# Two attention mixers re-ordered: pool products, window sums, scores, values and the first output products

## The chip, the cores and the metric

The kernel runs on one core of a Trainium2 chip. It is one launch, and the metric is its time on the device in microseconds (us). A core has engines that work side by side, each through its own queue in program order: TensorE (PE) for matrix products, VectorE (DVE), ScalarE (ACT) and GpSimd (POOL) for work on tiles, and SyncE (SP), whose queue issues the transfers of weights from memory. An instruction that needs the result of another engine waits on a semaphore, and everything behind it on its own engine waits with it. PE writes into PSUM, of which the kernel uses 8 banks of 128 x 512 numbers; all other tiles lie in SBUF.

## The reference

Two networks run one after the other on 512 tokens of width 1024. The change touches the mixers of the first network alone. It has two layers (DEPTH 2); each begins with a mixer block and ends with a gated feed-forward block:

```python
for l in range(DEPTH):
    h = rms_norm(x, g_mix_norm[l])
    z = h @ w_in[l]
    q_lat, kv_lat, k_rope, uv, pin = parts of z (256, 128, 32, 512, 256 wide)
    a  = mla_mixer(q_lat, kv_lat, k_rope, ...)     # 4 heads, causal softmax, values of 128 per head
    gm = sgu_mixer(uv, ...)                        # u * (causal 128x128 product over time of rms_norm(v) + b)
    po = pool_mixer(pin, w_pool[l], pool_scale[l])
    mix = concatenate([rms_norm(a, g), rms_norm(gm, g), rms_norm(po, g)])
    x = x + mix @ w_out[l]
    h = rms_norm(x, g_ffn_norm[l])
    x = x + (silu(h @ w_gate[l]) * (h @ w_up[l])) @ w_down[l]
```

`pool_mixer` takes four groups of 64 channels. Group g has a window of 2, 4, 8 or 16 tokens: the mean over the window (over fewer tokens at the start) minus the input, times a 64 x 64 matrix of the group, times a scale.

## The kernel before

All activations are kept turned: a tile holds 128 channels on its partitions and the 512 tokens along its free side. A weight product is made of three matmuls of 512 columns (lines 195 to 197): the weight and the activation are each split into a high and a low part, and high-high, low-high and high-low are added up in PSUM. Such a triple is called a product here. A weight arrives as a raw tile by a transfer of SP (three raw tiles at most), ACT makes its high part (L157) and DVE its low part (L158); the two together are a unit, of which five are alive at most. `plan_all` lists the units in the order in which they are wanted, and `get` and `done` split a few units ahead of the one in use. So a unit's place in the list also sets where its two splits stand in the queues of ACT and DVE.

`mixer(l)` writes out the order of everything else by hand, and each engine's queue is the order in which the code runs. It goes in stages:

1. The loop over four blocks of 128 tokens, `for b in range(4)`, makes q, k and v (lines 928 to 937, 18 matmuls of 384 columns for each b). ACT scales q and v out of PSUM (L940, L944), DVE scales k (L943), and ACT and POOL square them for their norms.
2. `pool_in(0)` scales the first pool tile (L959), and POOL forms its window sums by doubling shifts (L964, L965): a shifted addition and a short copy for each doubling. DVE then runs a reciprocal square root as a chain of ten small instructions (L978, then lines 247 to 256) for q, scales q, turns it by the rotary angles (lines 986 to 991) and splits three units.
3. PE meanwhile makes the 288 wide products (v of the gate and the rotary part of k, lines 1001 to 1003), then steps of the two gate tiles by `filler`, each step two products. `heads(0)` turns q and k of head 0 (L1055). ACT scales them out of PSUM (L1059).
4. The score loop: 16 items (h, b), head by block of queries, and 20 steps. Step i makes the score of item i (L1155) with its softmax (DVE maximum with mask L1158, ACT exponential L1162), scales the probabilities of item i-1 (L1170), turns those of item i-3 (L1178, evacuated by ACT at L1181) and multiplies item i-4 by v (L1194, a matmul of 128 columns for each pair of blocks). `side` hangs other work on steps: the eight steps of `second` (the product for the second pool tile, lines 195 to 197) in steps 0 to 3, the gate's spatial products, heads 1 to 3, `pool_mean` and `pool_out` (L1115) for the two pool tiles, and the norms of the gate tiles gm and the pool tiles po.
5. The output: six PSUM banks, first the products of gm and po (`mix[4:8]`) into the first two pairs, then those of the attention.

## Time and profile before

| what | value |
| --- | --- |
| median of 3 runs | 2565.69 us (2565.5 to 2567.38) |
| the profiled execution | 2565.37 us |
| its span in the trace | 2563.6 us |
| PE busy | 2538.0 us, 99% |
| DVE, ACT, POOL busy | 50%, 34%, 20% |
| mean granted clock of PE | 0.997 |
| mixer of layer 0 in the trace | about 20 to 145 us |
| mixer of layer 1 in the trace | about 541 to 650 us |

The span is from the first to the last instruction of the profiled execution; 1.8 us of its time lie outside. The timeline gives the start and length of an instruction or a group of like ones, and in brackets how long its engine sat idle before it and whose instruction ended that. A matmul's length overlaps the next one's, so the pace of PE is read from the distance of starts. In the windows view a clock of 1.00 means that the full 2.4 GHz was granted all the time; the lower level is 1.2 GHz.

### The profile page before, as it was taken

Reading aid. Unit: us, or ns where it says so; the run is one execution under the profiler, and the core shown is the slowest. Engines: PE = TensorE matmul, PEld = TensorE weight load, DVE = VectorE, ACT = ScalarE, POOL = GpSimd, SP = SyncE. Lnnn points to the kernel's source line nnn. Section 1 sums busy time; section 2 is a strip of 40 time slices with the busy share of each in tenths; the row PEclk is TensorE's granted clock in tenths of the full one; section 3 lists DMA queues with packets and bytes.
Section 4 is the critical chain, followed back from the end, with each engine's and each line's share of the span. In section 5 each row is a group of like instructions: output and inputs, shape, how many; then the busy total and the mean of one; then the engine's idle time right before and its main releaser. Section 6 shows DMA issues by size and latency. Waiting matters only on the chain.

```text
span 2563.6 us, 30126 instructions
## 1 busy us (share of the span) xinstructions
PE 2538.0 (99%) x12237; PEld 2106.6 (82%) x12237; DVE 1275.3 (50%) x1937; ACT 870.9 (34%) x1285; POOL 506.4 (20%) x409
## 2 busy tenths in 40 slices
PE   9999999999999999999999999999999999999998
PEld 7788888887888888888888888888888888888887
DVE  6855343468553434545433435653544445344345
ACT  5543232245432323323322334422222234233243
POOL 5412010124120101211330001252423331000011
PEclk9999999999999999999999999999999999999999
DMA  5032333220333232323333222423222213323321
GB/s 152 26 124 99 99 102 102 78 81 26 124 99 99 99 99 83 99 99 107 100 102 108 90 96 78 120 83 83 83 82 83 83 50 108 102 94 99 99 74 58
DMA packets 265219, 235.03 MB, mean 92 GB/s; under 512 B 9022, under 2 KB 262744, under 8 KB 265080
## 3 DMA queue, kind: packets, MB, share of 16 engines
q1 hardware_dynamic: 264264, 231.97, 28.9%
q8 instruction: 96, 1.57, 0.3%
q10 hardware_dynamic: 752, 1.12, 0.1%
q14 instruction: 43, 0.35, 0.0%
q0 software_dynamic: 64, 0.01, 0.0%
HBM read 230.98 MB, written 2.10 MB: 91 GB/s over the span
## 4 chain that ended last, share of the span: by engine, by line
PE 95%; DVE 1%; ACT 1%; issue 0%; DVEq 0%; ACTq 0%
PE ps L195 28%; PE ps L197 28%; PE ps L196 28%; PE v L1335 1%; PE v L1337 1%; PE v L1336 1%; PE ps L1361 1%; PE o L1394 1%; PE rows L287 1%; PE ps L1383 1%; PE o L1404 0%; PE ps L1357 0%; PE ps L1194 0%; PE ps L1155 0%; PE st L280 0%; PE ps L280 0%
## 5 line engine op out<-in xcount | busy, mean ns | idle before, releaser
L195 PE MATMUL ps<-h,wh 128*128 128x512 f32 x3248 | 1271.2, 391 | 0.7 <-ACT wh L157 0.7
L197 PE MATMUL ps<-h,wl 128*128 128x512 f32 x3248 | 1264.8, 389 | 1.4 <-DVE wl L158 1.4
L196 PE MATMUL ps<-l,wh 128*128 128x512 f32 x3248 | 1264.0, 389 | 0.1
L158 DVE TENSOR_TENSOR wl<-raw,wh 128x1024 fp32r<-128x1024 f32 (+4 forms) x466 | 579.6, 1253 | 837.0 <-ACT wh L157 835.2
L157 ACT ACTIVATE wh<-raw 128x1024 fp32r<-128x1024 f32 (+4 forms) x466 | 449.9, 986 | 1027.0 <-PE ps L196 984.4
L197 PEld LDWEIGHTS ps<-h,wl 128*128 128x128 f32 x3248 | 609.7, 188 | 130.5 <-DVE wl L158 2.7
L195 PEld LDWEIGHTS ps<-h,wh 128*128 128x128 f32 x3248 | 609.8, 188 | 127.5 <-issue 1.8
L196 PEld LDWEIGHTS ps<-l,wh 128*128 128x128 f32 x3248 | 610.0, 188 | 125.7 <-DVE l L234 0.5
L320 POOL TENSOR_TENSOR sq<-sq,sq 128x512 f32<-128x512 f32 x68 | 92.3, 1357 | 748.7 <-ACT sq L271 748.4
L679 POOL TENSOR_TENSOR th<-th,half 128x512 f32<-128x512 f32 x44 | 83.0, 1906 | 554.8 <-DVE th L678 554.8
L1307 POOL TENSOR_TENSOR sw<-sw,trig 32x512 f32<-32x512 f32 x48 | 74.8, 1559 | 286.9 <-DVE sw L1306 268.3
L647 DVE TENSOR_TENSOR x<-x,ps 128x512 f32<-128x512 f32 x144 | 97.9, 702 | 9.4 <-PE ps L197 9.4
L236 ACT ACTIVATE h<-x,vec 128x512 fp32r<-128x512 f32 x72 | 56.0, 778 | 102.4 <-DVE x L647 96.3
L234 DVE TENSOR_TENSOR l<-r,h 128x512 fp32r<-128x512 f32 x64 | 44.3, 693 | 88.0 <-ACT h L233 86.5
L237 DVE SCALAR_TENSOR_TENSOR l<-x,vec,h 128x512 fp32r<-128x512 f32 x72 | 58.0, 805 | 55.2 <-ACT h L236 55.1
L709 ACT ACTIVATE r<-r 128x512 f32<-128x512 f32 x64 | 40.5, 632 | 101.5 <-DVE r L708 101.5
L1314 POOL TENSOR_TENSOR qk<-qk,sw 32x512 f32<-32x512 f32 x32 | 59.5, 1860 | 2.5
L1370 ACT ACTIVATE P<-P,s 128x512 f32<-128x512 f32 (+1 forms) x32 | 22.1, 693 | 88.7 <-DVE s L1368 88.7
L1335 PE MATMUL v<-wh,h 128*128 128x512 f32 x128 | 51.0, 399 | 0.0
L271 ACT ACTIVATE sq<-x 128x512 f32<-128x512 f32 x79 | 48.8, 618 | 6.3 <-DVE x L728 6.3
L1337 PE MATMUL v<-wh,l 128*128 128x512 f32 x128 | 50.0, 390 | 0.0
L1336 PE MATMUL v<-wl,h 128*128 128x512 f32 x128 | 49.9, 389 | 0.0
(268 smaller groups left out, 1661.7 us busy)
## 6 DMA issues: line engine op xcount, KB each, us to landing
raw<-in_attn_w_qkv SPq DMA_DIRECT2D x72, 512.0 KB
raw<-in_mlp_w_up SPq DMA_DIRECT2D x32, 1024.0 KB
raw<-in_mlp_w_down SPq DMA_DIRECT2D x32, 1024.0 KB
raw<-in_w_gate SPq DMA_DIRECT2D x22, 1024.0 KB
raw<-in_w_up SPq DMA_DIRECT2D x22, 1024.0 KB
raw<-in_w_down SPq DMA_DIRECT2D x16, 1024.0 KB
raw<-in_sc_w_in SPq DMA_DIRECT2D x12, 1024.0 KB
raw<-in_w_out SPq DMA_DIRECT2D x16, 512.0 KB
```

The costliest lines, as they stand in the source:

```text
L157: nc.scalar.activation(out=hi, in_=raw, func=AF.Copy)
L158: nc.vector.tensor_tensor(out=lo, in0=raw, in1=hi.bitcast(F32), op=ALU.subtract)
L195: mm(out=ps, lhsT=wh, rhs=xh, start=start, stop=False)
L196: mm(out=ps, lhsT=wh, rhs=xl, start=False, stop=False)
L197: mm(out=ps, lhsT=wl, rhs=xh, start=False, stop=stop)
L320: nc.gpsimd.tensor_tensor(out=self.acc, in0=self.acc, in1=sq, op=ALU.add)
L647: self.nc.vector.tensor_tensor(out=x, in0=x, in1=ps, op=ALU.add)
L679: nc.gpsimd.tensor_tensor(out=t[i], in0=t[i], in1=half, op=ALU.mult)
L1307: pool.tensor_tensor(out=sw[0:32], in0=sw[0:32], in1=sinr, op=ALU.mult)
L1335: pe.matmul(out=pss[r], lhsT=xh, rhs=hi[:, k, :], start=first, stop=False)
L1336: pe.matmul(out=pss[r], lhsT=xh, rhs=lo[:, k, :], start=False, stop=False)
L1337: pe.matmul(out=pss[r], lhsT=xl, rhs=hi[:, k, :], start=False, stop=last)
```

## The change

In each of the two mixers:

- The unit of the second pool tile is planned ahead of the 288 wide units, and its eight products run in the q/k/v loop, two behind each b. The 24 matmuls leave the score loop.
- `pool_in(0)`, `pool_in(1)` and all window sums stand right behind the loop. POOL now has 14 instructions there instead of 4: in the last doubling of a tile the two halves of the partitions go apart, one as a copy of 64 x 512 (L974 of the new file), the other as an addition.
- `pool_mean` works on whole tiles (one DVE instruction of 128 x 512 and two short ones of POOL for each pool tile, instead of twice that on halves) and stands on DVE between the splits and the norm of k. `pool_out(0)` stands on PE ahead of the last three gate steps before `heads(0)`, `pool_out(1)` right ahead of `heads(0)`.
- The score's maximum becomes a minimum of the scaled and negated scores, so that the small DVE instruction between it and the exponential goes. The probabilities of the last block of queries are scaled by ACT instead of DVE.
- Probabilities are turned six steps behind their score instead of three, by block of keys: `turn(h, c)` takes block c of all later query blocks, and `values(h, c)` is one matmul of (4-c) x 128 columns. That makes 16 instead of 40 matmuls for a layer, with as many columns. The loop has 23 steps.
- The square of the attention output goes from POOL to ACT. The norms of gm and po share one chain on DVE (step 8), with the scaling and splitting of gm and po in steps 11 to 14 (before: 15 to 19).
- The first pair's products of gm and po (four steps of two products) stand in steps 16, 18, 20 and 22; the second pair's stand half ahead of and half behind the column sums of the attention's norm.

The diff, cut:

```diff
                 self.mm(ps, (hi[:, k, :], lo[:, k, :]), xs[k], start and k == 0, stop and k == n - 1)
         self.done(*[u for u, _, _ in us])
 
-    def pair_steps(self, pss, xs):
+    def pair_steps(self, pss, xs, stop=True):
 
         us = [self.get() for _ in pss]
         n = len(xs)
         for k in range(n):
             for ps, (u, hi, lo) in zip(pss, us):
...
             self.plan([(a["w_kv_up"][l], 0, 768)], 0, 1, [(0, 768)])
+            self.plan([(w, 1056, 128)], 0, 8, [(0, 128)])
             for k0, nk in ((0, 3), (3, 3), (6, 2)):
                 self.plan([(w, 672, 256), (w, 384, 32)], k0, nk, [(0, 288)])
             self.plan_cols(w, 8, 416, 256)
-            self.plan([(w, 1056, 128)], 0, 8, [(0, 128)])
...
+        pps.append(self.bank())
+        pool_steps = self.pair_steps(pps[1:], xs)
         for b in range(4):
...
             v.tensor_reduce(out=ssk[:, b * 4:b * 4 + 4], in_=t4, op=ALU.add, axis=mybir.AxisListType.X)
+            next(pool_steps)
+            next(pool_steps)
         self.done(uq, uk)
...
-            ss_ = [t]
-            for sh in ((1, 2), (1, 2, 4, 8))[i]:
-                s, o = self.T(name="sum"), ss_[-1]
-                pool.tensor_tensor(out=s[:, sh:], in0=o[:, sh:], in1=o[:, :512 - sh], op=ALU.add)
-                pool.tensor_copy(out=s[:, 0:sh], in_=o[:, 0:sh])
-                ss_.append(s)
-            sums.append(ss_[-2:])
...
+        def pool_sums(i):
+
+            o = pin[i]
+            win = ((1, 2), (1, 2, 4, 8))[i]
+            for sh in win:
+                s = self.T(name="sum")
+                last = sh == win[-1]
+                if last:
+                    pool.tensor_copy(out=s[0:64], in_=o[0:64])
+                p = slice(64, 128) if last else slice(0, 128)
+                pool.tensor_tensor(out=s[p, sh:], in0=o[p, sh:], in1=o[p, :512 - sh], op=ALU.add)
+                pool.tensor_copy(out=s[p, 0:sh], in_=o[p, 0:sh])
+                o = s
+            sums.append(o)
 
         pool_in(0)
+        pool_in(1)
+        pool_sums(0)
+        pool_sums(1)
...
-        gate_steps = self.pair_steps(ups, xs)
-
-        def second():
-            pps.append(self.bank())
-            yield from self.pair_steps(pps[1:], xs)
-
-        fill = [gate_steps] * 8 + [second()] * 8
+        fill = [self.pair_steps(ups, xs)] * 8
...
+        mm_ = []
+
+        def pool_mean(i):
+            m, s, c = self.T(name="m"), sums[i], i * 17
+            v.scalar_tensor_tensor(out=m, in0=s, scalar=self.counts[:, c + 16:c + 17], in1=pin[i], op0=ALU.mult, op1=ALU.subtract)
+            pool.tensor_tensor(out=m[:, 0:16], in0=s[:, 0:16], in1=self.counts[:, c:c + 16], op=ALU.mult)
+            pool.tensor_tensor(out=m[:, 0:16], in0=m[:, 0:16], in1=pin[i][:, 0:16], op=ALU.subtract)
+            mm_.append(m)
...
+        def pool_out(i):
+            ps = self.bank()
+            pe.matmul(out=ps, lhsT=pb[:, i * 128:(i + 1) * 128], rhs=mm_[i], start=True, stop=True)
+            t = self.T(name="po")
...
+        pool_mean(0)
+        pool_mean(1)
...
+        pool_out(0)
         filler(3)
+        pool_out(1)
         heads(0)
         filler(1)
...
+        def stats():
             ps = self.bank()
...
+            for c, j in ((0, "g"), (4, "p")):
+                self.columns(sgp[j], ps, c)
+            var = self.small(8)
+            v.tensor_scalar(out=var, in0=ps[:, 0:8], scalar1=1.0 / 256, scalar2=EPS, op0=ALU.mult, op1=ALU.add)
+            both = self.rsqrt(var)
+            fac["g"], fac["p"] = both[:, 0:4], both[:, 4:8]
...
-            mx, sm = self.small(1), self.small(1)
-            v.tensor_tensor_reduce(out=t[:, 0:n], in0=ps[:, 0:n], in1=self.causal[:, 512 - n:512], scale=1.0, scalar=-3e38,
-                                   op0=ALU.add, op1=ALU.max, accum_out=mx)
-            self.tick()
-            v.tensor_scalar(out=mx, in0=mx, scalar1=-scale, scalar2=None, op0=ALU.mult)
-            act.activation(out=t[:, 0:n], in_=t[:, 0:n], func=AF.Exp, scale=scale, bias=mx, accum_out=sm)
+            mn, sm = self.small(1), self.small(1)
+            v.tensor_tensor_reduce(out=t[:, 0:n], in0=ps[:, 0:n], in1=self.causal[:, 512 - n:512], scale=-scale, scalar=3e38,
+                                   op0=ALU.add, op1=ALU.min, accum_out=mn)
+            act.activation(out=t[:, 0:n], in_=t[:, 0:n], func=AF.Exp, scale=-1.0, bias=mn, accum_out=sm)
...
             v.reciprocal(out=sm, in_=sm)
-            self.tick()
-            v.tensor_scalar(out=t[:, 0:n], in0=t[:, 0:n], scalar1=sm, scalar2=None, op0=ALU.mult)
-            self.tick()
-
...
+            if b < 3:
+                v.tensor_scalar(out=t[:, 0:n], in0=t[:, 0:n], scalar1=sm, scalar2=None, op0=ALU.mult)
+            else:
+                act.activation(out=t[:, 0:n], in_=t[:, 0:n], func=AF.Copy, scale=sm)
...
-            for c in range(b + 1):
-                pe.transpose(blk(ps, c), blk(t, c), self.ident)
+            for b in range(c, 4):
+                pe.transpose(blk(ps, b), blk(prob[h, b][0], c), self.ident)
+            prob.pop((h, c))
...
-        def values(h, b):
-            if b == 0:
+        def values(h, c):
+            if c == 0:
...
-            t = ptt.pop((h, b))
-            for c in range(b + 1):
-                pe.matmul(out=blk(outs[h], b), lhsT=v4[:, c, h, :], rhs=blk(t, c), start=c == 0, stop=c == b)
-            if b == 3:
+            t = ptt.pop((h, c))
+            pe.matmul(out=outs[h][:, c * 128:], lhsT=v4[:, c, h, :], rhs=t[:, c * 128:], start=c == 0, stop=c == 3)
+            if c == 3:
...
-                s = self.T(name="sq")
-                pool.tensor_tensor(out=s, in0=o, in1=o, op=ALU.mult)
+                s = self.square(outs[h])
...
-                    pool.tensor_tensor(out=sa[0], in0=sa[0], in1=s, op=ALU.add)
+                    (v if h == 3 else pool).tensor_tensor(out=sa[0], in0=sa[0], in1=s, op=ALU.add)
...
-        side = {0: lambda: filler(3), 1: lambda: (filler(1), pool_mean(0)), 2: lambda: (filler(1), heads(1)),
-                3: lambda: (filler(3), pool_out(0)), 4: lambda: (filler(1), spatial(0), gate(0)),
-                5: lambda: (pool_in(1), spatial(1)), 6: lambda: gate(1),
-                7: lambda: (heads(2), pool_mean(1), squares(gm)), 8: lambda: heads(3), 10: lambda: pool_out(1),
-                11: lambda: stats("g"), 14: lambda: (stats("p"), rowsof("g")),
-                15: lambda: (scaled(gm, "g", v), rowsof("p")), 17: lambda: parts(gm, 4, "g_out_sgu"),
-                18: lambda: scaled(po, "p", v), 19: lambda: parts(po, 6, "g_out_pool")}
-        for i in range(len(items) + 4):
+        pss = []
+
+        def output(n):
+
+            if not pss:
+                pss.extend([self.bank(), self.bank()])
+                fill.extend([self.pair_steps(pss[0:2], mix[4:8], stop=False)] * 4)
+            filler(n)
+
+        side = {0: lambda: spatial(0), 1: lambda: (spatial(1), gate(0)), 2: lambda: (heads(1), gate(1)),
+                3: lambda: squares(gm), 6: lambda: heads(2), 8: stats, 9: lambda: heads(3),
+                10: lambda: (rowsof("g"), rowsof("p")), 11: lambda: scaled(gm, "g", v), 12: lambda: parts(gm, 4, "g_out_sgu"),
+                13: lambda: scaled(po, "p", v), 14: lambda: parts(po, 6, "g_out_pool")}
+        for i in range(len(items) + 7):
+            if 0 <= i - 6 < len(items):
+                turn(*items[i - 6])
             if i < len(items):
                 score(*items[i])
             if 0 <= i - 1 < len(items):
                 scale_p(*items[i - 1])
-            if 0 <= i - 3 < len(items):
-                turn(*items[i - 3])
-            if 0 <= i - 4 < len(items):
-                values(*items[i - 4])
+            if i in (16, 18, 20, 22):
```

On PE, layer 0, around the turning of head 0 (`ps`: PSUM tiles, `h` and `l`: parts of an activation, `wh` and `wl`: parts of a unit, `m`: the pool mean, `pb`: the pool matrix). Before:

```order
L197 MATMUL ps_831<-h_275,wl_678 128x512
L1055 MATMUL ps_918<-ident,q_562 96x128 x4
L1055 MATMUL ps_925<-ident,k_563 96x128 x4
L195 MATMUL ps_830<-h_285,wh_673 128x512
L196 MATMUL ps_830<-l_286,wh_673 128x512
L197 MATMUL ps_830<-h_285,wl_674 128x512
L195 MATMUL ps_831<-h_285,wh_677 128x512
L196 MATMUL ps_831<-l_286,wh_677 128x512
L197 MATMUL ps_831<-h_285,wl_678 128x512
L1155 MATMUL ps_951<-kT_930,qT_923 128x128
L195 MATMUL ps_959<-h_158,wh_796 128x512
```

The change:

```order
L197 MATMUL ps_876<-h_275,wl_709 128x512
L1043 MATMUL ps_979<-m_927,pb_360 128x512
L1089 MATMUL ps_986<-ident,q_562 96x128 x4
L1089 MATMUL ps_993<-ident,k_563 96x128 x4
L195 MATMUL ps_875<-h_285,wh_704 128x512
L196 MATMUL ps_875<-l_286,wh_704 128x512
L197 MATMUL ps_875<-h_285,wl_705 128x512
L195 MATMUL ps_876<-h_285,wh_708 128x512
L196 MATMUL ps_876<-l_286,wh_708 128x512
L197 MATMUL ps_876<-h_285,wl_709 128x512
L1168 MATMUL ps_1017<-kT_998,qT_991 128x128
L1117 MATMUL ps_1024<-wT_741,vn_1011 64x128 x4
```

`pool_out(1)` now stands ahead of the turning (and `pool_out(0)` 18 rows above it), and behind the first score come the spatial products instead of the second pool tile's.

On POOL behind the q/k/v loop (`pin`: pool tile, `sum`: window sums, `kr`, `kp`: rotary part of k). Before:

```order
L964 TENSOR_TENSOR sum_683<-pin_681 128x511
L965 COPY sum_683<-pin_681 128x1
L964 TENSOR_TENSOR sum_686<-sum_683 128x510
L965 COPY sum_686<-sum_683 128x2
L1035 TENSOR_TENSOR kr_860<-kr_860,s_551 128x64 x4
L1036 TENSOR_TENSOR kp_861<-kr_860 128x4x16
L1037 TENSOR_TENSOR kp_861<-kr_860 128x4x16
L1109 TENSOR_TENSOR m_982<-sum_683,counts 64x16
L1110 TENSOR_TENSOR m_982<-m_982,pin_681 64x16
```

The change, from the fourth of its instructions there:

```order
L976 TENSOR_TENSOR sum_719<-sum_716 64x510
L977 COPY sum_719<-sum_716 64x2
L976 TENSOR_TENSOR sum_723<-pin_714 128x511
L977 COPY sum_723<-pin_714 128x1
L976 TENSOR_TENSOR sum_726<-sum_723 128x510
L977 COPY sum_726<-sum_723 128x2
L976 TENSOR_TENSOR sum_729<-sum_726 128x508
L977 COPY sum_729<-sum_726 128x4
L974 COPY sum_732<-sum_729 64x512
L976 TENSOR_TENSOR sum_732<-sum_729 64x504
L977 COPY sum_732<-sum_729 64x8
L1035 TENSOR_TENSOR m_923<-sum_719,counts 128x16
```

All sums of both tiles, ten instructions more, and the first tile's short means now stand ahead of the work on k.

On DVE in the last steps with a score, 12 to 14 (`P`: probabilities, L1171: the minimum, L1154: scaling of gm and po, L237: low part of an activation). Before, at the end of the scores:

```order
L1168 RECIPROCAL s_1348<-s_1348 128x1
L1170 TENSOR_SCALAR P_1346<-P_1346,s_1348 128x384
L1141 TENSOR_TENSOR gm_1075<-gm_1075,rows_1391 128x512
L1141 TENSOR_TENSOR gm_1121<-gm_1121,rows_1391 128x512
L1168 RECIPROCAL s_1397<-s_1397 128x1
L1170 TENSOR_SCALAR P_1395<-P_1395,s_1397 128x512
L237 SCALAR_TENSOR_TENSOR l_1443<-gm_1075,vec,h_1442 128x512
L237 SCALAR_TENSOR_TENSOR l_1447<-gm_1121,vec,h_1446 128x512
L1141 TENSOR_TENSOR po_1045<-po_1045,rows_1423 128x512
L1141 TENSOR_TENSOR po_1265<-po_1265,rows_1423 128x512
L237 SCALAR_TENSOR_TENSOR l_1472<-po_1045,vec,h_1471 128x512
L237 SCALAR_TENSOR_TENSOR l_1476<-po_1265,vec,h_1475 128x512
```

The change:

```order
L1171 ISA P_1290,s_1291<-ps_1288,causal 128x128
L1171 ISA s_1291 128x1
L1179 RECIPROCAL s_1274<-s_1274 128x1
L237 SCALAR_TENSOR_TENSOR l_1299<-gm_1033,vec,h_1298 128x512
L237 SCALAR_TENSOR_TENSOR l_1303<-gm_1053,vec,h_1302 128x512
L1171 ISA P_1312,s_1313<-ps_1310,causal 128x256
L1171 ISA s_1313 128x1
L1179 RECIPROCAL s_1292<-s_1292 128x1
L1181 TENSOR_SCALAR P_1290<-P_1290,s_1292 128x128
L1154 TENSOR_TENSOR po_957<-po_957,rows_1262 128x512
L1154 TENSOR_TENSOR po_981<-po_981,rows_1262 128x512
L1171 ISA P_1331,s_1332<-ps_1329,causal 128x384
```

The scaling and splitting of gm and po stood behind the last maximum and now stand between the minima of head 3.

## Rows read from the trace of the kernel before

**Rows 1.** Page, part 4: shares of the chain that ended last.
```profile
PE 95%; DVE 1%; ACT 1%; issue 0%; DVEq 0%; ACTq 0%
```

**Rows 2.** Windows view, us from:to, length, busy (x instructions), clock, DMA, GB/s.
```profile
100.00:120.00 20.00, 18.02 (x123) 14.69 (x124) 15.84 (x63) 11.81 (x33) 10.27 (x12) 1.00 0.00 1
...
600.00:620.00 20.00, 17.35 (x119) 13.74 (x116) 16.28 (x43) 11.23 (x30) 14.64 (x19) 0.91 0.09 27
```

**Rows 3.** Waits of PE in layer 0's mixer: waiter, releaser, total us, times, longest.
```profile
PE ps L1194 <- ACT PT L1181: 2.8, 5, 1.4
PE ps L1155 <- ACT kT L1059: 2.0, 1, 2.0
PE ps L1055 <- DVE k L1047: 0.9, 1, 0.9
PE ps L935 <- ACT q L940: 0.5, 1, 0.5
PE ps L935 <- ACT v L944: 0.4, 1, 0.4
```

**Rows 4.** The same view, layer 1's mixer: its first line.
```profile
PE ps L1194 <- ACT PT L1181: 2.6, 4, 1.4
```

**Rows 5.** Timeline of PE: start us, us, what [idle before]; first products of stages.
```profile
42.08 0.42 PE L928 MATMUL ps<-wh,h 128*128 128x384 f32 x1
...
52.99 0.40 PE L1001 MATMUL ps<-wh,h 128*128 128x288 f32 x1
...
555.66 0.43 PE L928 MATMUL ps<-wh,h 128*128 128x384 f32 x1
...
564.46 0.38 PE L1001 MATMUL ps<-wh,h 128*128 128x288 f32 x1
...
577.29 0.40 PE L195 MATMUL ps<-h,wh 128*128 128x512 f32 x1
...
586.86 0.38 PE L1055 MATMUL ps<-ident,q 128*96 128x128 f32 x2
```

**Rows 6.** Timeline of DVE behind the q/k/v products, layer 0, last row layer 1.
```profile
61.84 0.69 DVE L978 TENSOR_SCALAR s<-s 128x16 f32<-128x16 f32 x1
...
62.77 1.01 DVE L249 TENSOR_TENSOR s<-s 128x16 f32<-128x16 f32 x1
...
63.81 0.18 DVE L250 TENSOR_TENSOR s<-s,s 128x16 f32<-128x16 f32 x1
...
65.28 1.76 DVE L981 TENSOR_TENSOR q<-q,s 128x1536 f32<-128x1536 f32 x1
...
69.51 2.80 DVE L158 TENSOR_TENSOR wl<-raw,wh 128x1024 fp32r<-128x1024 f32 x3
...
572.42 0.70 DVE L978 TENSOR_SCALAR s<-s 128x16 f32<-128x16 f32 x1
```

**Rows 7.** Timeline of POOL in layer 0: its second addition.
```profile
62.71 1.04 POOL L964 TENSOR_TENSOR sum<-sum 128x510 f32<-128x510 f32 x1
```

**Rows 8.** Timeline of ACT in layer 0's score loop.
```profile
107.08 0.68 ACT L271 ACTIVATE sq<-ps,vec 128x512 f32<-128x512 f32 x1
...
108.28 0.72 ACT L1162 ACTIVATE P<-P,s 128x512 f32<-128x512 f32 x1 [0.51 <-DVE s L1161]
```

**Rows 9.** Timeline of DVE in layer 0's score loop.
```profile
79.62 1.66 DVE L1071 SCALAR_TENSOR_TENSOR vn<-ps,s,gb 128x256 f32<-128x256 f32 x4
...
118.97 1.29 DVE L1141 TENSOR_TENSOR gm<-gm,rows 128x512 f32<-128x512 f32 x2
...
121.81 1.97 DVE L237 SCALAR_TENSOR_TENSOR l<-gm,vec,h 128x512 fp32r<-128x512 f32 x2 [0.38 <-ACT h L236]
```

**Rows 10.** Timeline of PE: layer 0's keys turned; its first output product; layer 1's score (1,0).
```profile
76.93 0.61 PE L1055 MATMUL ps<-ident,k 128*96 128x128 f32 x4 [0.91 <-DVE k L1047]
...
123.84 0.47 PE L195 MATMUL ps<-h,wh 128*128 128x512 f32 x1
...
610.55 0.49 PE L1155 MATMUL ps<-kT,qT 96*128 96x128 f32 x2 [2.04 <-ACT kT L1059]
```

More of the change, by code (lines that the diff above doesn't have):

```diff
@@ L220, in pair_steps @@
             for ps, (u, hi, lo) in zip(pss, us):
[L221 removed]
+                self.mm(ps, (hi[:, k, :], lo[:, k, :]), xs[k], k == 0, stop and k == n - 1)
             if k < n - 1:
@@ L1217, in mixer @@
                 scale_p(*items[i - 1])
-            if 0 <= i - 3 < len(items):
-                turn(*items[i - 3])
-            if 0 <= i - 4 < len(items):
-                values(*items[i - 4])
+            if i in (16, 18, 20, 22):
+                output(1)
+            if 0 <= i - 7 < len(items):
+                values(*items[i - 7])
             if i in side:
                 side[i]()
-        pss = [self.bank() for _ in range(6)]
-        self.pair(pss[0:2], mix[4:8], stop=False)
+        pss += [self.bank() for _ in range(4)]
+        steps = self.pair_steps(pss[2:4], mix[4:8], stop=False)
+        next(steps)
+        next(steps)
         sps = self.bank()
@@ L1231, in mixer @@
         ca = self.rsqrt(var)
-        self.pair(pss[2:4], mix[4:8], stop=False)
+        next(steps)
+        next(steps)
         row = self.rows(ca)
```

52 lines of the change are left out of this document (13 added, 39 removed).

## The prediction

> **What bounds the kernel now.** I read the page's chain first: PE holds 95% of it [rows 1], and its clock is nearly full, so the change can save only time in which PE waits or runs slow. The windows show where: in 100 to 120 us PE is busy 18.02 of 20, in 600 to 620 it is busy 17.35 with a granted clock of 0.91, that is partly at 1.2 and mostly at 2.4 GHz [rows 2]. DVE is busy 16 of 20 there, so the loop is short of slack, not of DVE throughput. The waits view then names what PE waits for. Layer 0: turned probabilities 2.8, keys out of ACT 2.0, k out of DVE 0.9, the q/k/v loop 0.5 + 0.4 [rows 3]. Layer 1: 2.6 [rows 4], and 2.0 before the first score of head 1 [rows 10].
>
> **What can be gained.** The q/k/v loop of layer 0 takes 52.99 - 42.08 = 10.91 us, in layer 1 564.46 - 555.66 = 8.80 [rows 5], so its waits with their small gaps are worth 2.1. With the 0.9 before k and 4.8 in the score loop layer 0 holds 7.8. Layer 1 holds 4.6, and the low clock in 600 to 620 costs 20 x 0.09 = 1.8: together 6.4. If all of this went and nothing came, 14.2 us would be saved, 0.55%.
>
> **Work that only moves.** A product takes (586.86 - 577.29) / 14 = 0.68 us, since 14 stand between these two rows [rows 5]. The eight pool products are 5.47 wherever they stand, and so are the eight output products pulled into steps 16 to 22. Value matmuls become fewer but have the same columns, and the rows of the loop go by columns; I take zero. The two pool_out matmuls only leave the loop. POOL's square of the attention and DVE's 512 wide scaling go to ACT, which is busy 11.8 of 20 in 100 to 120 [rows 2] and hides them except in the late steps below. The moved weight unit reorders splits and transfers, with no more of either; layer 0's loop starts some 0.25 us later for the larger split ahead of it, covered by the products inside. Tail and merged norms: the two halves of the second output pair are 2.7 us each and cover a chain of ten small DVE steps (0.21 each, from 63.81 to 65.28 in seven [rows 6]); zero.
>
> **Step 1, the q/k/v loop: -2.1.** ACT and DVE set its pace in layer 0. Two products behind each b put 1.37 us of PE work where it waited. Layer 1 had no wait, so nothing there.
>
> **Step 2, pool_out(0) ahead of heads(0): +4.2 and +2.3.** PE reaches it after 8.80 + 5.47 + 12.83 (the 288 wide products, 564.46 to 577.29 [rows 5]) + 5.47 (four gate steps) = 32.6 us: at 74.6 in layer 0. What it needs is the last of a long DVE queue. That chain began at 61.84 before [rows 6]; a second pool_in (some 0.6), a 576 wide split that now comes behind the loop (some 0.9) and the later start of the loop put it at about 63.8. Without hindrance: chain 2.1, q and rotation 4.2 (65.28 to 69.51), three splits of 512 some 2.1 (2.80 is for four such widths [rows 6]), the mean and its two short POOL steps 1.3, so 73.5, before PE comes. But POOL now has six additions, two half copies and six short copies there, about 9 us, to 71.5. While one runs, DVE's small steps stand still: 0.69 and 1.01 instead of 0.18 [rows 6], each ending with an addition of 1.04 [rows 7]; between two additions about two steps get through. Ten steps then need five additions with their copies at 1.25 each, 6.3 instead of 2.1, and q waits for the last addition, 1.1 more. The mean is there at 73.5 + 4.2 + 1.1 = 78.8, PE waits 4.2. Bounds: 0, if the copies leave DVE free, and 6.0, if DVE's long steps also hold POOL up. In layer 1 the chain began at 572.42, 16.8 us behind the first product against 19.8 in layer 0 [rows 5, 6], but DVE must now follow a loop 5.47 longer, which gives back 1.1 of the 3.0: 2.3, bounds 0 and 4.2. Behind it on PE wait three gate steps and head 0; no other engine is short of them.
>
> The Trainium skill ("SBUF — State Buffer", Who interferes with whom) says that a VectorE instruction with two SBUF inputs and a GpSimd instruction that reads SBUF exclude each other, and that whichever began holds the other up for its whole length. The blocked rows agree; that POOL is held up too no row of this stretch shows, since its additions keep their 1.04. By the full rule step 2 would be at its upper ends, 6.0 + 4.2, and the total 3.7 us more.
>
> **Step 3, k of head 0: +0.9 each, -0.9 in layer 0.** With 4 us more of PE work ahead of it, k is ready when PE comes, so the old 0.9 [rows 3] goes. But its turning takes a PSUM bank that pool_out(1) just filled, and that ACT frees after a scaling and a square of 0.68 each at most [rows 8], less 0.43 of q's turning: 0.8 to 1.1.
>
> **Step 4, the start of the score loop: +4.4 each.** Before, pool products stood between the first scores; now nothing does. The spatial products wait for vn, a split and 1.66 us on DVE [rows 9], against 2.8 us at most since k's turning: 1.5. Score (1,0) waits for k of head 1 behind three exponentials on ACT: 1.8 by the queue order, near the 2.0 that the same wait had [rows 3]. turn(0,0) needs the score (0,3) of three PE entries earlier to pass maximum, exponential (0.72 [rows 8]), reciprocal and ACT's scaling: 1.1. Bounds 3 and 5.
>
> **Step 5, the late steps: +4.8 each.** Before, gm and po were scaled and split behind the last maximum. Now the four scalings (1.29 for two) and four low parts (1.97 for two [rows 9]), 6.5 us of DVE, stand between the minima of head 3, with four high parts and two norm rows on ACT among its exponentials. Minima and scalings of head 3 are some 3.5 us more, so DVE has 10 us in steps 11 to 14, in which PE has some 7 of scores, turns and values. PE waits at values (1,1), (1,3), (2,0), (2,1), (2,2) and at turn(2,0): following the three queues by the rows' lengths I find 0.65 + 0.65 + 0.85 + 2.25 + 1.65 + 0.4 = 6.4. Such a walk misses short gaps on both sides: before's loop, 46.9 us from 76.93 to 123.84 [rows 10], is 3.3 longer than its matmuls and waits added up. I count half of that against the 6.4: 4.8, bounds 2.6 (DVE's excess alone) and 6.4.
>
> **Sum.** Layer 0: -2.1 + 4.2 - 0.9 + 0.9 + 4.4 + 4.8 - 4.8 (the loop's old waits) = +6.5. Layer 1: 2.3 + 0.9 + 4.4 + 4.8 - 4.6 - 1.8 = +6.0. The profiled execution has 2565.4 us, its span 2563.6 and 1.8 outside; 2565.4 + 12.5 = 2577.9, and with the median 0.3 above it, **2578**. All terms at their lower ends give -1.4 and 0: 2564. All at their upper ends, with the clock dip staying: +10.7 and +12.1: 2588.
>
> **Rivals.** *The old waits go and few new ones come (faster).* Turning six steps behind gives the softmax twice the time, the cause of most waits in rows 3 and 4. If the copies leave DVE free (step 2: 0) and the late queues drain inside the six steps (step 5: 0), with step 4 at the spatial wait alone, 1.5: layer 0 +2.4 - 7.8, layer 1 +2.4 - 6.4: 2565.7 - 9.4 = 2556. It decides from new waits under 7.1 us a layer. For it: the lag is generous for heads 0 to 2, and the small step behind the maximum is gone. Against it: DVE's blocked steps are in the trace, and the late work is queued ahead of the exponentials that the last turns need.
>
> *About no change.* Step 2 near zero, the loop's new waits just replacing the old: 2562 to 2570.
>
> *The clock falls behind the new waits.* A wait of 2.04 left the clock at 1.00 in 100 to 120, while in layer 1 the same wait stands in the window with 0.91 [rows 2, 3, 10]. The waits of step 2 and 5 may each cost such a 1.8: two to four of them make 2582 to 2585. The Trainium skill ("TensorE: Matmul & The Clock Gate", HAM oscillation) has waits in a loop throttle PE again and again; these rows show it in one of two cases.
>
> *The change doesn't do what it says:* the pool products might still trail the loop if their unit came late; its transfer starts where that of a 288 wide unit did, so I give that nothing of its own.
>
> **Chances.** Forecast 0.45, low clock 0.22, about no change 0.2, faster rival 0.13. A difference under 0.2%, 5.1 us, is about what a measurement of this kernel can't tell from none, so same is 2560.6 to 2570.8. The forecast's lower tail falls into it: faster 0.13, same 0.22, slower 0.65. The range leaves out the faster rival and the worst: 2561 to 2588.
>
> **What would show it.** Right: PE idle some 4 us before L1043 in layer 0 and 2 in layer 1, released by POOL or DVE; POOL additions back to back with DVE's chain stretched to 6 us beside them; no wait left at L935; waits at the values matmul in the last head's steps. Wrong: a chain of 2 us beside the sums, or the pool mean there before PE; a first score row without waits; values without waits from step 12 on. A q/k/v loop of over 15 us would mean that the moved unit came late.

## The result: 0.7% slower

| | before | the change |
|---|---|---|
| median, us | 2566.53 (2565.5 to 2568.17) | 2585.66 (2580.3 to 2587.12) |
| profiled execution, us | 2565.37 | 2586.89 |
| its span, us | 2563.6 | 2585.1 |
| mean granted clock of TensorE (PE) | 0.997 | 0.993 |

The ratio is 1.0072, with a 95% interval of 1.0059 to 1.0084: slower, and clear of the 0.2% that the prediction took as the least that such a measurement can tell. The forecast was 2578, the range 2561 to 2588.

The chain that ended last, in the page of the changed kernel (part 4), holds what [rows 1] did not: DVE with three per cent and POOL with one.

```profile
PE 94%; DVE 3%; ACT 1%; POOL 1%; issue 1%; DMA 0%; ACTq 0%; DVEq 0%; POOLq 0%
```

The waits view of the changed kernel, for PE, layer 0's mixer (waiter, releaser, total us, times, longest):

```profile
PE ps L1202 <- ACT PT L1192: 4.1, 4, 1.7
PE ps L1043 <- POOL m L1036: 3.6, 1, 3.6
PE ps L1189 <- ACT P L1183: 1.3, 2, 1.1
PE ps L1168 <- ACT kT L1093: 1.2, 1, 1.2
PE ps L1117 <- DVE vn L1107: 1.1, 1, 1.1
PE ps L1089 <- ACT sq L271: 0.9, 1, 0.9
```

Of the five waits of [rows 3] those on k, q and v are gone, those on PT and kT now stand at other products, and four are new: 12.2 us against 6.6. In layer 1 the six are the same, but for 1.7 at L1043: 10.3 against the 4.6 of [rows 4, 10]. Waits thus grew by 11.3. The timeline of PE (start, length, what, idle before) says where they lie:

```profile
42.39 0.42 PE L930 MATMUL ps<-wh,h 128*128 128x384 f32 x1
...
57.04 0.38 PE L1016 MATMUL ps<-wh,h 128*128 128x288 f32 x1
...
79.14 1.13 PE L1043 MATMUL ps<-m,pb 128*128 128x512 f32 x2 [3.63 <-POOL m L1036]
...
88.18 0.64 PE L1089 MATMUL ps<-ident,k 128*96 128x128 f32 x4 [0.92 <-ACT sq L271]
...
120.95 0.33 PE L1189 MATMUL ps<-ident,P 128*128 128x128 f32 x1 [0.26 <-ACT P L1183]
...
122.34 0.49 PE L1202 MATMUL ps<-PT,v 128*128 128x128 f32 x2 [0.41 <-ACT PT L1192]
...
124.47 1.12 PE L1202 MATMUL ps<-PT,v 128*128 128x512 f32 x2 [0.46 <-ACT PT L1192]
...
128.80 0.91 PE L1202 MATMUL ps<-PT,v 128*128 128x384 f32 x2 [1.59 <-ACT PT L1192]
...
131.49 1.22 PE L1202 MATMUL ps<-PT,v 128*128 128x256 f32 x2 [1.66 <-ACT PT L1192]
...
567.45 0.43 PE L930 MATMUL ps<-wh,h 128*128 128x384 f32 x1
...
581.82 0.38 PE L1016 MATMUL ps<-wh,h 128*128 128x288 f32 x1
```

From the first q product of layer 0 to that of layer 1 it is 567.45 - 42.39 = 525.1 us, where [rows 5] have 513.6: layer 0 became 11.5 longer. What follows, 2585.1 - 567.45 = 2017.7 against 2007.9, became 9.7 longer. That is some 10 us more than the growth of the waits, and the windows view (from:to, length, busy by engine, granted clock, DMA share, GB/s) shows it:

```profile
80.00:100.00 20.00, 16.66 (x90) 11.39 (x88) 12.44 (x36) 8.07 (x18) 5.66 (x9) 0.91 0.09 26
100.00:120.00 20.00, 18.82 (x96) 13.87 (x96) 10.05 (x42) 13.27 (x34) 2.85 (x3) 0.83 0.00 1
120.00:140.00 20.00, 15.62 (x62) 10.24 (x61) 8.10 (x20) 11.76 (x28) 2.56 (x2) 0.91 0.00 1
...
620.00:640.00 20.00, 18.71 (x102) 14.16 (x102) 11.33 (x47) 14.11 (x37) 4.11 (x4) 0.91 0.01 1
640.00:660.00 20.00, 15.62 (x57) 10.21 (x55) 8.10 (x20) 11.41 (x27) 2.56 (x2) 0.83 0.00 0
```

Here 100 to 120 has a busier PE than in [rows 2], 18.82 against 18.02, and gets less done: its clock is 0.83 instead of 1.00. At 20 us for each share of clock that is missing, layer 0 loses 20 x (0.09 + 0.17 + 0.09) = 7.0 and layer 1 20 x (0.09 + 0.17) = 5.2, where before lost 1.8 [rows 2]: 10.4 more. Finer windows of the same kernel show stretches near half speed (1.2 GHz), each behind PE's idle time:

```profile
76.00:80.00 4.00, 0.86 (x3) 0.49 (x3) 3.79 (x13) 0.00 (x0) 1.61 (x6) 1.00 0.41 131
80.00:84.00 4.00, 4.00 (x12) 3.03 (x11) 3.22 (x8) 1.27 (x2) 1.31 (x5) 0.57 0.00 0
...
100.00:104.00 4.00, 2.92 (x11) 2.04 (x11) 2.42 (x8) 2.64 (x7) 2.85 (x3) 0.58 0.01 4
```

So the 21.5 us between the two spans are about half waits and half clock. The second half is an estimate from the windows; the first run below tests it. The clock varies from run to run: the changed kernel's run of 2580.3 us had a mean of 0.996, those of 2584.4, 2586.9 and 2587.1 had 0.993.

### The profile page after: what moved, and what is told of

Its sections match the earlier page's. It is cut to its first block, busy times and chain, and to the rows that moved or that the text cites. A ratio compares the mean times of both kernels' runs of the same rounds, so it can differ in the third digit from the quotient of the medians.

```text
span 2585.1 us, 29866 instructions
## 1 busy us (share of the span) xinstructions
PE 2546.5 (99%) x12141; PEld 2103.5 (81%) x12141; DVE 1257.5 (49%) x1875; ACT 881.2 (34%) x1301; POOL 492.4 (19%) x395
## 4 chain that ended last, share of the span: by engine, by line
PE 94%; DVE 3%; ACT 1%; POOL 1%; issue 1%; DMA 0%; ACTq 0%; DVEq 0%; POOLq 0%
PE ps L195 28%; PE ps L197 28%; PE ps L196 28%; PE v L1353 1%; PE v L1355 1%; PE v L1354 1%; PE ps L1379 1%; PE o L1412 1%; PE rows L287 1%; PE ps L1401 1%; PE o L1422 0%; PE ps L1375 0%; PE ps L1202 0%; DVE wl L158 0%; PE ps L1168 0%
## 5 line engine op out<-in xcount | busy, mean ns | idle before, releaser
L158 DVE TENSOR_TENSOR wl<-raw,wh 128x1024 fp32r<-128x1024 f32 (+3 forms) x466 | 577.8, 1249 | 855.6 <-ACT wh L157 854.5
L157 ACT ACTIVATE wh<-raw 128x1024 fp32r<-128x1024 f32 (+3 forms) x466 | 449.9, 986 | 1026.9 <-PE ps L196 982.3
L237 DVE SCALAR_TENSOR_TENSOR l<-x,vec,h 128x512 fp32r<-128x512 f32 x72 | 58.0, 805 | 55.5 <-ACT h L236 55.4
```

What stands on the lines that cost most here:

```text
L157: nc.scalar.activation(out=hi, in_=raw, func=AF.Copy)
L158: nc.vector.tensor_tensor(out=lo, in0=raw, in1=hi.bitcast(F32), op=ALU.subtract)
```

## The experiments

All times are medians; the kernel before stood at 2566.0 to 2566.7 beside them. A line number is that of the kernel named.

**What the idle time of PE costs besides itself: e4_busy.** On the changed kernel:

```diff
+        def warm(ps, n):
+            for _ in range(n):
+                pe.matmul(out=ps, lhsT=xs[0][0][:, 0:128], rhs=xs[0][0], start=True, stop=True)
...
+            if i == 0:
+                warm(ps, (15, 7)[l])
```

and `warm(ps, 5)` ahead of `spatial(0)`, `score(1, 0)` and `turn(0, 0)`.

> The changed kernel with matmuls of 512 columns without use put in front of four waits of PE in each layer, into the bank that the waiting matmul then overwrites, about as long as the wait: 15 and 7 before pool_out(0), 5 each before the first spatial product, score (1,0) and turn(0,0). No work is taken away, so all waits on other engines end when they did. Theory (idle time of PE lowers its clock, and this costs beside the waits): granted clock 1.00 at 80 to 108 us and at 620 to 628, which saves 1.9 + 3 in layer 0 and some 2 in layer 1: about 2579. Rival (the clock falls for another reason, or only the waits matter): the clock rows stay and the time is 2585 or, by the matmuls added, above.

Measured: 2577.62 (2576.86 to 2578.69), ratio 1.0044 (1.0029 to 1.0059), 8.0 less than the change, as the theory had it. The timeline of PE shows the longest wait filled, and the windows view the clock:

```profile
74.67 3.56 PE L1043 MATMUL ps<-h 128*128 128x512 f32 x15
78.41 1.12 PE L1049 MATMUL ps<-m,pb 128*128 128x512 f32 x2 [0.17 <-POOL m L1036]
```

```profile
80.00:100.00 20.00, 18.77 (x109) 13.14 (x109) 13.34 (x38) 9.77 (x23) 7.16 (x9) 1.00 0.08 27
100.00:120.00 20.00, 18.78 (x106) 13.24 (x105) 12.34 (x49) 14.16 (x36) 0.63 (x1) 1.00 0.00 1
120.00:140.00 20.00, 16.80 (x75) 12.78 (x74) 6.64 (x17) 10.62 (x23) 2.56 (x2) 0.91 0.08 27
```

The product behind the wait, L1049, starts only 0.7 us earlier (78.41 against 79.14), since the layer's first product already did (41.74 against 42.39); no work was taken away, yet 8 us are gone. Keeping PE busy keeps its clock, and that is the 8 us: of the windows that lost clock one is left, 120 to 140 with 0.91, and the two profiled executions differ by 9.9 where the windows give 10.4. With the clock kept, the change stands at the forecast's 2578. That it does so to within 1 us is partly luck: the forecast's waits were 3.5 too long, and it counted no low clock at all, where e4 still has 1.8.

**Which wait takes the clock: e12_busy_first.** Of e4 only the first filling, in layer 0 alone: `warm(ps, (15, 0)[l])`.

> The changed kernel with 15 matmuls without use ahead of the first pool product of layer 0 alone, into the bank which that product then overwrites; all other waits stay. Theory A (each low stretch of the clock follows the waits right ahead of it): of layer 0's low stretches only that in 80 to 84 us goes, 0.43 of 4 us, so about 1.7 us off the changed kernel's 2585.7, 2584 in the median, and the granted clock from 100 to 108 and from 128 to 136 us stays below 1. Theory B (the low stretches follow the whole row of waits, which the first long one opens): the layer's other low stretches go too, about 6.8 us in all, 2579. Rival (the wait itself gets longer, because the products of no use keep the reader of the bank or the q chain waiting): 2586 or more.

Measured: 2582.56 (2580.16 to 2586.52), ratio 1.0068 (1.0052 to 1.0084). In the profiled run (2580.89) the clock of layer 0 is 1.00 in every window, though its other waits are as long as in the change, to the tenth; that is theory B, and the 6.0 us between the two profiled executions fit its 6.8. Layer 1, where nothing was touched, begins 6.4 us earlier than in the change and has its two low stretches at the same waits as the change, on P and on the last PT, but with their lengths exchanged: about 7 and 3 us here, about 3 and 7 there, the same loss in all. Windows view of this kernel, one window of layer 0 and one of layer 1:

```profile
100.00:120.00 20.00, 18.78 (x107) 13.44 (x106) 11.99 (x47) 14.48 (x37) 1.12 (x1) 1.00 0.00 0
...
616.00:620.00 4.00, 3.98 (x15) 3.17 (x16) 1.53 (x5) 2.64 (x7) 1.72 (x2) 0.50 0.00 0
```

The median, 3.1 us below the change, lies between the two theories, and its four runs span 6.4 us: the medians differ by less than the runs of either kernel. So one trace speaks for theory B, and how much clock a single wait takes is left open; that the row of waits takes it is what e4 shows.

**What the sums on POOL do: e3_no_sums.** On the changed kernel; this one leaves the window sums out, the means being formed from the pool tiles themselves.

```diff
         def pool_sums(i):
 
             o = pin[i]
+            sums.append(pin[i])
+            return
```

> The changed kernel without the window sums: the pool means are formed from the pool tiles themselves, all other instructions stay. Theory (POOL's additions block DVE's small steps): the chain of ten is back at 2.1 us, the waits of 3.6 and 1.7 at pool_out(0) go, with the low clock behind the first: 2585.7 - 7 = about 2579. Rival (DVE's queue is too long by itself): a wait of 3 us stays in layer 0, 2584 and above.

Measured: 2575.29 (2571.05 to 2578.77), ratio 1.0033 (1.0021 to 1.0044), 10.4 less than the change. The timeline of DVE, first of the changed kernel, then of this one:

```profile
64.40 0.17 DVE L993 TENSOR_SCALAR s<-s 128x16 f32<-128x16 f32 x1
...
69.11 1.00 DVE L256 SCALAR_TENSOR_TENSOR s<-s,s 128x16 f32<-128x16 f32 x1
70.15 1.76 DVE L996 TENSOR_TENSOR q<-q,s 128x1536 f32<-128x1536 f32 x1
...
77.25 1.41 DVE L1034 SCALAR_TENSOR_TENSOR m<-sum,counts,pin 128x512 f32<-128x512 f32 x2
```

```profile
64.05 0.16 DVE L995 TENSOR_SCALAR s<-s 128x16 f32<-128x16 f32 x1
...
65.92 0.17 DVE L256 SCALAR_TENSOR_TENSOR s<-s,s 128x16 f32<-128x16 f32 x1
66.12 1.76 DVE L998 TENSOR_TENSOR q<-q,s 128x1536 f32<-128x1536 f32 x1
...
71.87 1.41 DVE L1036 SCALAR_TENSOR_TENSOR m<-pin,counts 128x512 f32<-128x512 f32 x2
```

Ten small steps take 5.75 us beside the sums and 2.07 without. The means come 5.4 earlier, and no wait is left at `pool_out(0)` in either layer, 5.3 us of the 10.4. The rest I read as clock, which this run alone doesn't prove: the profiled run (2571.07) has 1.00 in every window of both mixers, with the other waits of the change unaltered, while four of the six runs had a lower mean clock. The theory's 2579 counted less of the clock coming back.

**Sums elsewhere: e2_pool_in_loop.** On the changed kernel, both tiles' sums behind the rotary work on POOL, `pool_mean` in steps 2 and 4, `pool_out` in 3 and 5.

> The changed kernel with one part undone: window sums behind the rotary work on POOL, pool_mean in steps 2 and 4 and pool_out in steps 3 and 5 of the score loop, as the old kernel had them in the loop. Theory (the mean at the end of DVE's hindered queue holds PE, and the squares hold the bank of k): the waits at pool_out(0), 3.6 and 1.7, and at k of head 0, 0.9 each, go, and the low clock behind the first (1.9): 2585.7 - 9 = about 2577. Rival (the work only moves into a loop that has no slack at its start): the loop's early waits grow by 4 us or more, 2583 and above.

Measured: 2590.48 (2588.09 to 2591.13), ratio 1.0092 (1.0075 to 1.0109). A miss. The waits view, layer 0:

```profile
PE ps L1087 <- DVE k L1079: 4.6, 1, 4.6
PE ps L1041 <- POOL m L1034: 4.6, 2, 3.4
```

and the timeline of DVE and of POOL beside it:

```profile
78.81 0.99 DVE L255 SCALAR_TENSOR_TENSOR s<-s,s 128x20 f32<-128x20 f32 x1
...
80.63 2.13 POOL L976 TENSOR_TENSOR sum<-sum 64x504 f32<-64x504 f32 x1
...
81.57 1.73 DVE L1079 TENSOR_TENSOR k<-kp,s 128x512 f32<-128x512 f32 x1
```

The sums now hold up k's norm where they held up q's, and the means are late again: the same sums, 10.2 us of POOL in layer 0 here, found another chain. The rival's time came true, but half of the new waits stand ahead of the loop, at k.

**The late steps: e1_late.** On the changed kernel:

```diff
-                10: lambda: (rowsof("g"), rowsof("p")), 11: lambda: scaled(gm, "g", v), 12: lambda: parts(gm, 4, "g_out_sgu"),
-                13: lambda: scaled(po, "p", v), 14: lambda: parts(po, 6, "g_out_pool")}
+                10: lambda: (rowsof("g"), rowsof("p")), 15: lambda: (scaled(gm, "g", v), parts(gm, 4, "g_out_sgu")),
+                16: lambda: scaled(po, "p", v), 17: lambda: parts(po, 6, "g_out_pool")}
...
-            if i in (16, 18, 20, 22):
+            if i in (18, 19, 20, 21):
```

> The changed kernel with one part altered: gm and po are scaled and split only behind the last minimum of head 3 (steps 15 to 17 instead of 11 to 14), and the first pair's output products stand in steps 18 to 21 instead of 16, 18, 20, 22. Theory (the late waits come from that work standing on DVE and ACT ahead of head 3's minima and exponentials): the five waits of the last steps, 4.4 us in each layer of the changed kernel, fall under 1, and with them the stretch at a lower clock behind them (about 1.5 in layer 0, 3 in layer 1); 2585.7 - 7 - 4 = about 2574. Rival (the last turns come too soon behind the last scores whatever stands between): 3 us or more of waits stay in each layer, 2582 to 2586.

Measured: 2578.25 (2577.55 to 2582.45), ratio 1.005 (1.0035 to 1.0065): 7.4 less, 4.3 short of the theory. Of the late waits one large one stays (timeline of PE):

```profile
127.51 0.88 PE L1202 MATMUL ps<-PT,v 128*128 128x256 f32 x2 [2.27 <-ACT PT L1192]
```

Its PT stands on ACT behind the two high parts of the gate results. In layer 0 the 4.4 us of late waits became 2.6, so 1.8 of them came from the late work's old place in the queues, and the rest now stands behind its new one. Two layers of that are 3.6 of the 7.4; the rest is not shown to be clock, but the runs other than the profiled one had a mean clock of 0.995 or 0.996 where most runs of the change had 0.993.

**The products between q, k and v alone: e5_qkv_only.** On the kernel before, the unit moved and its eight products put into the q/k/v loop, as in the change; the eight `filler` entries of the second pool tile in the score loop have then nothing to do, and all else stays.

> The old kernel with one part of the change alone: the second pool tile's unit planned early and its eight products in the q/k/v loop, so that none are left as cover in steps 0 to 3 of the score loop; everything else as it was. Theory (the loop gains its 2.1 us in layer 0, k of head 0 another 0.9, but the scores lose 5.4 us of cover at their start and show early waits as in the changed kernel, some 3.4 in each layer, with a low clock behind them): 2566 - 3 + 7 + 3 = about 2573. Rival (the cover was not needed, DVE and ACT keep up): 2563.

Measured: 2575.73 (2575.07 to 2576.96), ratio 1.0037 (1.0023 to 1.005). Waits of PE, layer 0:

```profile
...
PE ps L1113 <- POOL m L1108: 1.8, 1, 1.8
PE ps L1153 <- DVE vn L1069: 1.0, 1, 1.0
PE ps L1053 <- ACT qT L1057: 0.8, 1, 0.8
```

The lines left out are the old waits on PT and kT. Those on q, k and v go (1.8), and three new ones of 3.6 stand there, in layer 1 too, where nothing was to be gained: +5.4. The clock is 0.91 in 80 to 100 and 0.83 in 600 to 620, 20 x (0.09 + 0.17) - 1.8 = 3.4 more than before. This part alone costs over 9 us, and these two are 8.8 of it: the products it takes out of the score loop had covered the three waits.

**The turning alone: e8_scores_only.** The changed kernel's scores, turning by block of keys, values and merged norm, with all pool work where the kernel before has it, the scalings in steps 15 to 18 and the output's products in 19 to 22.

> The other half alone: the new scores, softmax, turning by block of keys and values, with all pool work (products, sums, means) where the old kernel has it, and gm and po scaled and split in steps 15 to 18. Theory (the pool work ahead of the scores and the late work cost the time, the new turning itself does not): no wait at pool_out, early waits as covered as before, 1 to 2 us of late waits; 2566 - 2 x 3 = about 2560. Rival (turning six steps behind and by block of keys delays the last head by itself): 2568 and above.

Measured: 2564.93 (2563.46 to 2567.64), ratio 0.9995 (0.9986 to 1.0005). So the loss of the change is not in its new turning. One large wait is left in each layer; the timelines of DVE and PE:

```profile
99.04 1.86 DVE L1034 SCALAR_TENSOR_TENSOR m<-sum,counts,pin 128x512 f32<-128x512 f32 x1 [2.19 <-POOL sum L973]
...
102.35 0.33 PE L1185 MATMUL ps<-ident,P 128*128 128x128 f32 x1 [2.91 <-ACT P L1179]
```

DVE stands at the means until POOL has the sums, and the minima of the scores stand behind it.

**Taking that wait away: e9_mean_later, e10_in_earlier, e11_mean_first.** Each builds on the one before. The table of steps, from e8 to e11:

```diff
-                3: lambda: (filler(3), pool_out(0)), 4: lambda: (spatial(0), gate(0)),
-                5: lambda: (pool_in(1), pool_sums(1), spatial(1)), 6: lambda: (heads(2), gate(1)),
-                7: lambda: (pool_mean(1), squares(gm)), 9: lambda: heads(3), 10: lambda: pool_out(1),
-                12: stats, 14: lambda: (rowsof("g"), rowsof("p")), 15: lambda: scaled(gm, "g", v),
+                3: lambda: (filler(3), pool_out(0)), 4: lambda: (spatial(0), gate(0), pool_in(1), pool_sums(1)),
+                5: lambda: spatial(1), 6: lambda: (heads(2), gate(1)),
+                8: lambda: pool_mean(1), 9: lambda: (heads(3), squares(gm)), 11: lambda: pool_out(1),
+                13: stats, 14: lambda: (rowsof("g"), rowsof("p")), 15: lambda: scaled(gm, "g", v),
```

> The e8 version (the changed kernel's scores, turning and values, the pool work where the kernel before has it, the scaling of the pool and gate results and their parts in steps 15 to 18, the output's first products in steps 19 to 22), with the means of the second pool tile moved from step 7 to step 9, its product from step 10 to 11 and the norm's factors from step 12 to 13. Theory (in e8 the 2.9 us wait of TensorE on ScalarE's P at turn(1,0), once in each layer, came from VectorE standing at the means until POOL's sums were done; two steps of about 2.3 us cover it): that wait goes in both layers, 2 x 2.9, and the low clock of one stretch with it, 1.8, so e8's 2564.9 becomes about 2558, with bounds 2557 to 2561. Rival (POOL's sums are as late for the next who needs them: TensorE then stands at the pool product or at the norm's columns instead): 2563 to 2566, with a wait on POOL's m or on a sum of squares of 2 us or more in steps 11 to 13.

Measured: 2565.18 (2562.82 to 2567.33), ratio 0.9993 (0.9984 to 1.0002). The rival: PE waits 2.4 at the pool product instead, since POOL does the gate results' squares ahead of the means' 16 columns.

> As e9, and the second pool tile's input product and window sums one step earlier (step 4 instead of 5). Theory (POOL's sums are what is late; started about 2.3 us earlier they end about that much earlier): the same as e9 where e9's cover is enough, about 2558, and up to 2 us less where e9 still waits on the means. Rival (the earlier sums share their time with VectorE's q and k products of the heads and with the gate's steps, which hold one another up, as in the run with the sums behind the rotary work): a new wait of 1.5 us or more on a gate product or on kT in steps 4 to 7 of each layer, 2561 to 2566.

Measured: 2563.02 (2561.18 to 2566.72), ratio 0.9986 (0.9977 to 0.9995). Sums that start a step earlier take only 0.3 off the wait; what is left lies behind them, with the squares.

> As e10, with the second tile's means in step 8 instead of 9 and the squares of the gate results in step 9 instead of 7, so that POOL's two 16-column steps of the means stand ahead of its two squares and their sum (in e9 those squares, 2.09 and 1.28 us from 101.66, stood between the sums and the means, and TensorE waited 2.4 us for them at the pool product; in e10 2.1). Theory (POOL's order makes that wait): it goes in both layers, 2 x 2.1, and e10's 2563.0 becomes about 2559, bounds 2557 to 2561. Rival (VectorE then stands at the means in step 8 until the sums are done, as in e8, or the squares are late for the norm's columns at step 13): a wait of 1 us or more on P or on the columns' sums, 2562 to 2565.

Measured: 2561.36 (2560.75 to 2563.42), ratio 0.9981 (0.9972 to 0.9991). Waits of PE, first line of either layer:

```profile
PE ps L1198 <- ACT PT L1188: 2.0, 2, 1.6
```

The wait on POOL's m is gone, and most of it came back at the value products, 1.6 and 0.4: DVE now stands 1.00 at the means. That is the rival's mechanism at another place. The version is 0.19% faster than the kernel before, with no overlap between the runs of the two, and 24 us faster than the change; it takes from the change the turning and the late products, and leaves pool work in the score loop.

**Two attempts that only moved waits.** e6_heads_early, on the kernel before:

```diff
-                5: lambda: (pool_in(1), spatial(1)), 6: lambda: gate(1),
-                7: lambda: (heads(2), pool_mean(1), squares(gm)), 8: lambda: heads(3), 10: lambda: pool_out(1),
+                5: lambda: (heads(2), pool_in(1), spatial(1)), 6: lambda: gate(1),
+                7: lambda: (pool_mean(1), squares(gm)), 8: lambda: heads(3), 10: lambda: pool_out(1),
```

> The old kernel with head 2 turned in step 5 of the score loop instead of step 7. Theory (the wait of 2.04 us for the keys of head 2 comes from turning it one step ahead of its first score, and the low clock at 611 to 615 us in layer 1 comes from that wait): both waits and the low clock go, 2566 - 4.1 - 1.8 = about 2560. Rival (ACT is late by then whatever the order, the wait moves to the next turned probabilities): 2565 to 2567.

Measured: 2568.94 (2567.11 to 2570.93), ratio 1.0009 (1.0 to 1.0019). The waits on kT are gone, those on PT grew from 2.8 and 2.6 to 4.8 and 4.9. A miss, and slower than the rival too: with the old lag of three steps the score loop waits for its softmax with head 2 in either place.

e7_mixed, on the changed kernel: the first tile's sums alone ahead of the score loop, the second tile's in step 3, the means in steps 1 and 7, the pool products in steps 3 and 8, one more gate step behind head 0 as cover, the late work as in e8.

> The changed kernel with the pool products in the q/k/v loop and its scores, but with the first tile's sums alone ahead of the scores, the second tile's in step 3, the pool means and products in steps 1 to 8, two gate steps kept as cover behind head 0, and gm and po scaled and split in steps 15 to 18. Theory (no sums beside the norm of q and k, cover at the start, no late work ahead of head 3's minima): no wait at pool_out and k of head 0, early waits under 1.5, late waits under 1.5 in each layer and no low clock; 2566 - 2.1 - 0.9 - 2 x 2 - 1.8 = about 2557. Rival (the gate steps taken from ahead of head 0 make PE wait for k, and POOL's second sums block the scalings of P): 2566 and above.

Measured: 2577.59 (2576.21 to 2578.69), ratio 1.0043 (1.0028 to 1.0058). A miss by 20 us. The first tile's product does not wait any more; the second's does, 4.8 in layer 0 and 6.5 in layer 1 (timelines of POOL and of PE, layer 0):

```profile
101.35 1.26 POOL L1129 TENSOR_TENSOR sq<-sq,sq 128x512 f32<-128x512 f32 x1
...
103.14 2.07 PE L1041 MATMUL ps<-m,pb 128*128 128x512 f32 x2 [4.76 <-POOL m L1034]
```

The second tile's means stand on POOL behind its sums, a gate product and the squares of the gate results with their sum, which end at 102.6; e9 above has the same order, and e11 its cure.

## Why the prediction was right in sign and short in size

- **Step 1** (the q/k/v loop, -2.1 and 0). It took 57.04 - 42.39 - 5.47 = 9.2 us without its pool products, 1.7 less than [rows 5] give, and in layer 1 8.9, no less. Right within 0.4; but e5 shows that the same products had been worth more in the score loop. The sum had this in step 4, not here.
- **Step 2** (+4.2 and +2.3). PE came at 75.5 (forecast 74.6) and the mean at 79.1 (78.8): waits of 3.6 and 1.7. Ten DVE steps took 5.75, five of them 0.47 to 1.06 and each ending with a step of POOL, as the two rows in [rows 6] had suggested. e3 confirms the cause. No row of before showed whether POOL is held up too. It is; the timeline of POOL in the changed kernel, a copy of 64 x 512 among DVE's small steps and its like beside DVE's q product at 70.15:

```profile
64.60 0.65 POOL L974 COPY sum<-sum 64x512 f32<-64x512 f32 x1
...
70.28 2.10 POOL L974 COPY sum<-sum 64x512 f32<-64x512 f32 x1
```

  The Trainium skill ("SBUF — State Buffer", Who interferes with whom) says that a DVE instruction with two SBUF inputs and a POOL instruction that reads SBUF contend, and that the order of issue decides which of them waits; here the trace agrees, 2.10 against 0.65. The upper end of 6.0 was not reached all the same: the sums ended at 74.1 and DVE took them up at 77.25.
- **Step 3** (+0.9). Measured 0.92 in both layers, released by ACT's square, as said.
- **Step 4** (+4.4). 1.1 for vn, 1.2 for kT, 1.1 for P at turn(0,0): 3.4. The 1.8 for kT at score (1,0) leaned on a wait of 2.0 that was misread: in the kernel before it stands behind the third turning of k, at the first score of head 2, and so does its twin of layer 1 in [rows 10] (timeline of PE, before):

```profile
97.56 0.60 PE L1055 MATMUL ps<-ident,k 128*96 128x128 f32 x4
100.20 0.49 PE L1155 MATMUL ps<-kT,qT 96*128 96x128 f32 x2 [2.04 <-ACT kT L1059]
```

- **Step 5** (+4.8, with the walk itself at 6.4). 0.26 + 0.41 + 0.46 + 1.59 + 1.66 = 4.4, at turn(2,0) and four of the five value products named; values (1,1) had no wait. Right to half a microsecond.
- **The old waits** all went from their places, as assumed.
- **The clock: the step that failed.** The sum took 1.8 off layer 1 for a low stretch that would go with its waits, and put nothing in for new ones. Measured: 10.4 more than before instead of 1.8 less, so 12.2 off. The waits, 14.3 in the sum without that 1.8, came to 10.8 when the measured steps above replace its terms, which gave 3.5 back; together they make the 9 us between the forecast of 2577.9 and the profiled 2586.9. The rival that the clock falls behind the new waits was what happened, at 2585.7 where it said 2582 to 2585. It came this close by two errors: it counted 3.6 to 7.2 us of clock for 12.2, on waits that were 3.5 too long. That the range held the result is owed to its upper end, 2588, which had no new loss of clock in it either. The rival had 0.22, because a wait of 2.0 in layer 0 had the full clock beside it and its twin in layer 1 had not [rows 2, 3, 10]. That was read as a chance for each long wait; the runs show a loss for a row of them, of which most are about 1 us. In the traces it went with the first wait of a layer: a layer of e3 or e12 without the wait at `pool_out(0)` kept its clock through the same later waits, while one with it lost 5 to 7 us; but other executions of e3 lost clock without it. The Trainium skill ("TensorE: Matmul & The Clock Gate", HAM oscillation) describes waits in a loop that lower the clock again and again, there waits for transfers; here they are waits for other engines, and e4 agrees that the clock falls behind them, with 8.0 us.
- **The faster rival** needed new waits under 7.1 us a layer; they were 12.2 and 10.3. Its reason (twice the lag for the softmax) holds, as e8 shows, where the waits on PT of layer 0 fell from 2.8 to 0.8, but only with the pool work left between the scores and the late work behind them.

## What to carry to other kernels

Matmuls that need nothing are cover: before moving them out of a loop in which PE waits for other engines, count which waits they stand in front of, since 5.5 us of products taken from there cost more (e5) than the 2 us of waiting which they filled elsewhere. Price a row of short waits on TensorE at between one and two times their length, and test it by filling them with matmuls of no use: here 11.3 us more of waits cost some 10 of clock besides, while the 11.2 that the kernel before already had cost 1.8. When a wait goes, look at what is next in the queue that released it: e6, e7, e9 and e11 each traded a wait for another, and of these rows of trades only that from e8 to e11 was worth something, 3.6 us by the medians.

## What the runs showed of the hardware

- With the same program the clock fell in some executions and not in others: of e3's six runs two had a mean of 0.998 and 2571.1 us, the others 0.995 or 0.996 and 2574.5 to 2578.8. Only one execution has a trace, so that their waits were the same is not shown. Medians of a few runs of such a kernel are uncertain by some us.
- VectorE and GpSimd hold each other up in turn: beside back to back additions of 1.03 to 1.04 on POOL every second small DVE step took 0.99 to 1.06 instead of 0.17. In e2 it was also a step with one tensor operand: L251, 128 x 20, took 0.99 from 76.33 on and ended with an addition of 1.04 that POOL had begun at 76.25.
